# Hybrid decoder step: prompt's attention moved beside the sample's, the output projection beside the sample's products, the sample's dot products into the query stage

## Chip, cores and metric

One core of one Trainium2 chip runs the whole program. The metric is device time of one execution in microseconds (us); lower is better. Engines: PE (TensorE, matmuls and transposes), DVE (VectorE), ACT (ScalarE), POOL (GpSimd, which also issues the indirect gathers) and SP (SyncE, which issues all plain loads and stores).

## What is computed

One layer of a decoder over 256 prompt tokens and 8 x 4 sample tokens, all float32. Cut to what matters here:

```
proj = x @ w_in
y_r  = rwkv_time_mix(proj)        # 16 heads x 64, recurrence over tokens
y_n  = nsa_mix(proj)              # 16 query heads, 4 KV heads; compressed, selected, window; gated sum
x    = layer_norm(ALPHA * x + concat(y_r, y_n) @ w_out)
q    = x @ peer_wq                # then two top-16 searches over 128 keys, 16 experts a head
h    = gelu(x . u_tab[expert]);   f = sum(gate * h * v_tab[expert])
x    = layer_norm(ALPHA * x + f)
```

Prompt and sample do all of it with the same weights. The prompt's compressed, selected and window branches run over its own 256 keys, the sample's over 2048 cached tokens, gathered by page.

## The kernel before, in words

The program is one function, `hybrid_decode_step`. Its parts are Python generators that issue instructions and yield a cost; `weave((gen, weight), ...)` takes the next step of the generator that is furthest behind its weight, so parts are issued in turns. A scheduler of the framework then orders each engine's queue with a model of times, with the program's order as the priority. On the chip each queue runs in order. Tiles of one name share `bufs` slots; the first writer of a tile waits until the slot's last reader is done. PSUM has 8 banks, handed out by name: `banks(sa=2, sao=1, ...)`.

The stretches of the span (times in us from its start) that the change touches:

1. W3 (550 to 793): three parts woven. `late` is the sample's attention (30 of its 40 units of 256 keys each run here: transposes at L881 into bank `sa`, scores L894 into `pb`, softmax L898 to L908, transposes L913 into `pb`, values L921 into `sao`). `sample_states` and `sample_steps` (L1140 to L1270) are the sample's recurrence, bank `ss`. `take(prompt, NP3)` is 30 of the 84 steps of the prompt's recurrence (`prompt_steps`, L970 to L1133), bank `pa`. Cached keys come by gathers on POOL (L422, tile `co`) into a ring of 4 + NCX = 7 buffers.
2. W4 (793 to about 1117): again three parts woven. The prompt's last 18 steps; `prompt_attention` (L594 to L690), which for each half of the tokens (`qt`), each KV head (`kvh`) and each of its 4 query heads (`g`) makes scores for the selected and window branch (L654, bank `sa`), masks and takes maxima (L659), exponentiates (L664), transposes (L670, bank `sa`), copies (L672) and multiplies with values (L676, bank `sao`); after 4 heads the bank is scaled and added (L678 to L684). The results, transposed, go to `YN` (L690). `sample_chain` (L1386 to L1480): the sample's gates, its output projection (L1416, all 32 weight tiles of `w_out` read by themselves), layer norm, query product (L1416 again, `w_q`), choice of experts (`choose`, `settle`), and 64 gathers of 128 rows of `u_tab` (L422, tile `cw`, 5 buffers), each multiplied with x and summed: 52 on DVE (L1476), every fifth on POOL and ACT (L1473, L1474).
3. out (927 to 1182, overlapping W4): `out_part(0, BV)` and then `out_part(8, YN)`, the prompt's output projection. Each of 32 weight tiles is split into a high part (ACT, L1595) and a low part (DVE or POOL, L1596) and takes 12 matmuls (L1601, bank `pa`). Before it the prompt's gates (L1614, L1615).
4. ln1 (1182 to 1222): the prompt's layer norm, its transposes, stores of x.
5. wq (1222 to 1380): the prompt's queries (L1721) on PE. After each head, `choose` and `settle` on DVE (L1274 to L1327), with a product on POOL in them (L1320). The next stage (dense, L1744) writes `AW` (L1764), 128 KB per partition, where the tiles of wq were; its first write waits for the last `settle`.

Afterwards come dense (to 1855), weigh (to 2132) and V (to 2699). SBUF is a stack on a left and a right side: a pool opened after another has closed takes its place, so its first loads wait for the last reader there.

Of the kernel before, what the change touches and what calls it, by code (L numbers as in the profile page):

```python
# [38 lines left out]
OFFC = 5  # L39
# [5 lines left out]
NCX = 3  # L45
# [4 lines left out]
NP3 = 30  # L50
# [19 lines left out]
def _const_table():  # L70
# [23 lines left out]
    g5["bmask"] = bm  # L94
# [54 lines left out]
def hybrid_decode_step(ctx: ExitStack, tc: tile.TileContext, a, outs, dbg=None):  # L149
# [98 lines left out]
    KT = nq([P, 2, 2, NT], "KT")  # L248
    VS, VW = ([nq([P, 256], f"{nm}{t}") for t in range(2)] for nm in ("vs", "vw"))
# [343 lines left out]
    def prompt_attention():  # L593
# [12 lines left out]
        for qt in range(2):  # L606
# [39 lines left out]
            for kvh in range(4):  # L646
                kp, par = kvh // 2, kvh % 2
                po = bank("sao")
                su = np_([P, 4, 2], "su", bufs=2)
                for g in range(4):  # L650
                    yield 1
                    pb = bank("sa")
                    for br in range(2):
                        pe.matmul(pb[:, 256 * br:256 * br + nk], QT[hs[par], kp, g, tok], KT[hs[par], br, kp, :nk],  # L654
                                  start=True, stop=True)
                    Sm = np_([P, 2, 256], "Sm", bufs=2)
                    m2 = np_([P, 2], "m2", bufs=3)
                    for br in range(2):
                        ve.tensor_tensor_reduce(out=Sm[:, br, :nk], in0=pb[:, 256 * br:256 * br + nk],  # L659
                                                in1=C2("causal")[:, 256 - nk:256], scale=1.0, scalar=NEG,  # L660
                                                op0=OP.add, op1=OP.max, accum_out=m2[:, br:br + 1])
                    ve.tensor_scalar(m2, m2, -1.0, None, op0=OP.mult)
                    for br in range(2):
                        sc.activation(Sm[:, br, :nk], Sm[:, br, :nk], AF.Exp, bias=m2[:, br:br + 1],  # L664
                                      accum_out=su[:, g, br:br + 1])
                    pb = bank("sa")
                    for br in range(2):
                        for kt in range(qt + 1):
                            o = 256 * br + 128 * kt
                            pe.transpose(pb[:, o:o + 128], Sm[:, br, 128 * kt:128 * kt + 128], ident)  # L670
                    PTs = np_([P, 2, 256], "PTs", bufs=2)
                    sc.copy(PTs[:, :, :nk], pb.rearrange("p (a b) -> p a b", a=2)[:, :, :nk])  # L672
                    for br in range(2):
                        for kt in range(qt + 1):
                            o = 128 * g + 64 * br
                            pe.matmul(po[:, o:o + 64], PTs[:, br, 128 * kt:128 * kt + 128],  # L676
                                      (VS, VW)[br][kt][:, 64 * kvh:64 * kvh + 64], start=(kt == 0), stop=(kt == qt))
                ve.reciprocal(su, su)  # L678
                ve.tensor_tensor(su, su, Gt[:, 4 * kvh:4 * kvh + 4, 1:3], OP.mult)
                to = np_([P, 4, 2, 64], "to", bufs=2)  # L680
                ve.tensor_tensor(to.rearrange("p g r d -> p (g r) d"), po.rearrange("p (n d) -> p n d", n=8),
                                 su.rearrange("p g r -> p (g r)")[:, :, None].to_broadcast([P, 8, 64]), OP.mult)
                for br in range(2):
                    ve.tensor_tensor(O[:, 4 * kvh:4 * kvh + 4, :], O[:, 4 * kvh:4 * kvh + 4, :], to[:, :, br, :], OP.add)  # L684
            for q in range(2):
                pb = bank("sa")
# [473 lines left out]
    def sample_steps(sm):  # L1160
# [69 lines left out]
        for j in range(8):  # L1230
            pb = bank("ss")
            for h in range(2):
                uvm = sm([64, 8, 64], "uvm", bufs=2, tag="PR")
                gp.tensor_tensor(uvm, UVt[:, j, None, 64 * h:64 * h + 64].to_broadcast([64, 8, 64]),
                                 C5("bmask")[:64, :, None].to_broadcast([64, 8, 64]), OP.mult)
# [5 lines left out]
        for b in range(8):  # L1241
# [3 lines left out]
            S1 = sm([P, 4, P], "S1", bufs=2, tag="S0")  # L1245
# [10 lines left out]
        Yq, Yv = sm([P, 256], "Yq"), sm([P, 256], "Yv")  # L1256
# [4 lines left out]
        rsqrt(sm, Yq, Yv, "sg")  # L1261
# [123 lines left out]
    def sample_chain(cx):  # L1385
# [53 lines left out]
        x4, X1s = cx([P, D], "x4"), cx([P, 16, 32], "X1s")  # L1439
# [4 lines left out]
        for g in range(4):  # L1444
            sy.dma_start(x4[32 * g:32 * g + 32, :], X1D[NPR:NT, :])
# [16 lines left out]
        hd = cx([P, 2, 32], "hd")  # L1462
# [5 lines left out]
        for s_ in range(32):  # L1468
# [559 lines left out]
```

## Time and profile before

| what | us |
|---|---|
| median of 3 runs | 2686.79 |
| lowest, highest | 2673.55, 2705.59 |
| profiled execution: its own time | 2701.19 |
| profiled execution: span of its instructions | 2699.3 |

Busy over the whole span: PE 89%, DVE 73%, ACT 39%, POOL 49%. In the views below PE is the matmuls and PEld the weight loads beside them; PEclk is the granted clock of TensorE as a share of 2.4 GHz (0.5 is its lower level, 1.2 GHz). A PE that is busy in the records may still be slow, because matmuls overlap and because the clock is low.

### The profile page before, as it was taken

The numbers are of one execution on the slowest core, as the hardware profiler recorded it, in microseconds if no ns is written. First come the engines' busy times: TensorE is split into PE (matmuls) and PEld (weight loads), VectorE is DVE, ScalarE is ACT, GpSimd is POOL, SyncE is SP. The second block draws the span as 40 slices with busy tenths as digits, with TensorE's granted clock in tenths as the row PEclk, the third lists the DMA queues.
The fourth block names the chain that finished last, engine by engine and source line by source line (L and its number), as shares of the span: only waits on it lengthen the run. The fifth ranks groups of instructions, "written<-read, shape, count | busy, mean of one in ns | idle before, by whom it ended". The sixth has DMA issues, their size and how long they took to land.

```text
span 2699.3 us, 47864 instructions
## 1 busy us (share of the span) xinstructions
PE 2394.6 (89%) x17636; PEld 2005.0 (74%) x17636; DVE 1962.0 (73%) x4360; ACT 1046.3 (39%) x1958; POOL 1333.8 (49%) x1348
## 2 busy tenths in 40 slices
PE   6998899989879998659979999998679799999996
PEld 5877788756556656438879999997667588878885
DVE  3699864347533438784988887888986589888888
ACT  2443223332321323331134444443456544444543
POOL 3688642224210006763654444445556377767772
PEclk9999999978988588679989999998789899999998
DMA  5688866662647566777569999998668599999994
GB/s 170 197 262 261 242 201 188 222 187 101 210 149 269 158 209 222 257 253 207 168 218 351 352 350 346 348 352 276 225 213 298 193 336 321 328 341 321 328 322 176
DMA packets 346317, 683.49 MB, mean 253 GB/s; under 512 B 81230, under 2 KB 204443, under 8 KB 345019
## 3 DMA queue, kind: packets, MB, share of 16 engines
q1 hardware_dynamic: 251172, 344.67, 39.3%
q0 software_dynamic: 94912, 335.77, 35.4%
q8 instruction: 139, 2.28, 0.3%
q14 instruction: 94, 0.77, 0.1%
HBM read 664.77 MB, written 23.88 MB: 255 GB/s over the span
## 4 chain that ended last, share of the span: by engine, by line
PE 61%; DVE 14%; DMA 8%; issue 5%; POOL 3%; ACT 2%; SPq 1%; DVEq 0%; POOLq 0%; ACTq 0%
PE pb L1953 19%; PE ph L1762 13%; PE pt L1757 4%; PE pj L388 3%; PE pj L1721 2%; DVE rows L1687 2%; PE pa L1601 2%; PE pa L1002 1%; PE pa L1835 1%; PE sa L881 1%; PE fs L1853 1%; PE ss L1416 1%; PE px L1805 1%; PE pa L1059 1%; DMA co<-in_cache_sel_kv,sidx 1%
## 5 line engine op out<-in xcount | busy, mean ns | idle before, releaser
L422 POOL DMA_INDIRECT rows<-in_peer_u,gi x256 | 308.4, 1205 | 320.5 <-DVE rows L1687 284.4
L422 POOL DMA_INDIRECT rq<-in_peer_v,gi x256 | 374.9, 1464 | 171.6 <-issue 92.3
L1762 PE MATMUL ph<-XHd,uh 128*128 128x256 f32 x1024 | 306.5, 299 | 15.9 <-ACT AW L1764 15.9
L1687 DVE SCALAR_TENSOR_TENSOR rows<-rows,x1a 128x1024 f32<-128x1024 f32 x256 | 308.1, 1231 | 0.0
L1762 PE MATMUL ph<-XHd,ul 128*128 128x256 f32 x1024 | 297.5, 291 | 6.9 <-DVE ul L1574 6.9
L1762 PE MATMUL ph<-XLd,uh 128*128 128x256 f32 x1024 | 290.8, 284 | 0.0
L388 PE MATMUL pj<-XH,wl 128*128 128x288 f32 (+1 forms) x752 | 234.1, 312 | 33.1 <-DVE wl L383 17.2
L1573 ACT CAST uh<-pt 128x512 fp32r<-128x512 f32 x256 | 150.2, 587 | 271.8 <-PE ph L1762 271.0
L1574 DVE TENSOR_TENSOR ul<-pt,uh 128x512 fp32r<-128x512 f32 x256 | 176.5, 690 | 90.1 <-ACT uh L1573 86.9
L388 PE MATMUL pj<-XH,wh 128*128 128x288 f32 (+1 forms) x752 | 230.0, 306 | 7.6 <-DVE BV L767 4.8
L388 PE MATMUL pj<-XL,wh 128*128 128x288 f32 (+1 forms) x752 | 226.8, 302 | 0.0
L1953 PE MATMUL pb<-vl,ah 128*128 128x512 f32 x768 | 216.8, 391 | 1.3 <-DVE vl L1947 1.3
L1953 PE MATMUL pb<-vh,al 128*128 128x512 f32 x768 | 216.2, 390 | 0.0
L1953 PE MATMUL pb<-vh,ah 128*128 128x512 f32 x768 | 197.7, 393 | 18.6 <-ACT vh L1946 18.6
L1762 PEld LDWEIGHTS ph<-XHd,uh 128*128 128x128 f32 x1024 | 197.6, 193 | 16.2 <-ACT AW L1764 16.2
L1762 PEld LDWEIGHTS ph<-XHd,ul 128*128 128x128 f32 x1024 | 197.0, 192 | 7.6 <-DVE ul L1574 7.6
L1762 PEld LDWEIGHTS ph<-XLd,uh 128*128 128x128 f32 x1024 | 197.7, 193 | 0.0
L1927 DVE SCALAR_TENSOR_TENSOR fP<-rq,ge,fP 128x512 f32<-128x512 f32 x254 | 189.5, 746 | 4.3 <-DMA rq<-in_peer_v,gi 1.8
L381 ACT CAST wh<-wraw 128x512 fp32r<-128x512 f32 (+1 forms) x188 | 114.2, 616 | 185.5 <-PE pj L388 115.2
L1953 PEld LDWEIGHTS pb<-vh,ah 128*128 128x128 f32 x768 | 145.6, 190 | 49.5 <-ACT vh L1946 19.3
L388 PEld LDWEIGHTS pj<-XH,wl 128*128 128x128 f32 (+1 forms) x752 | 145.0, 193 | 49.0 <-DVE wl L383 24.4
L1953 PEld LDWEIGHTS pb<-vl,ah 128*128 128x128 f32 x768 | 144.8, 189 | 32.3 <-DVE vl L1947 2.1
(840 smaller groups left out, 5719.2 us busy)
## 6 DMA issues: line engine op xcount, KB each, us to landing
ur<-in_peer_u SPq DMA_DIRECT2D x128, 512.0 KB
wraw<-in_w_in SPq DMA_DIRECT2D x152, 256.0 KB
cw<-in_w_out SPq DMA_DIRECT2D x32, 512.0 KB
cw<-in_peer_wq SPq DMA_DIRECT2D x32, 512.0 KB
wraw<-in_w_out SPq DMA_DIRECT2D x32, 512.0 KB
wraw<-in_peer_wq SPq DMA_DIRECT2D x32, 512.0 KB
wraw<-in_w_in SPq DMA_DIRECT2D x64, 128.0 KB
co<-in_state_win_kv SPq DMA_DIRECT2D x16, 512.0 KB
```

The costliest lines, as they stand in the source:

```text
L381: sc.copy(wh[:, :, :n], w[:, :, :n])
L388: pe.matmul(pb[:n, :nt], wi[:, k, :n], xi[(o + k) // 8][:, (o + k) % 8, :nt], start=(o + k == 0 and wi is wh and xi is xh), stop=(o + k == ...
L422: gp.indirect_dma_start(out=dst, out_offset=None, in_=rows_, in_offset=bass.IndirectOffsetOnAxis(ap=ix, axis=0))
L1573: sc.copy(xh, pb)
L1574: return ve.tensor_tensor(xl, pb, xh.bitcast(F32), OP.subtract)
L1601: pe.matmul(acc[t], xi[:, e, P * t:P * t + P], wi[:, e, :], start=(k == e == n_ == 0), stop=(k == 6 and e == 1 and n_ == 2))
L1687: i_ = ve.scalar_tensor_tensor(r_, r_, 1.0, X1a[t], op0=OP.mult, op1=OP.mult, accum_out=h_)
L1721: pe.matmul(pb[:, :NPR], w[:, k, :], XT[:, o + k, :], start=(o + k == 0), stop=(o + k == 15))
L1757: pe.transpose(pb[:, 128 * e:128 * e + 128], w[:, 512 * q + 128 * e:512 * q + 128 * e + 128], ident)
L1762: mm = pe.matmul(ph[:, :NPR], wi[:, e, :], xi[:, 4 * q + e, :NPR], start=(q == 0 and e == 0 and wi is wh and xi is XHd), stop=(q == 1 and ...
L1927: ve.scalar_tensor_tensor(fP[t], r_, w_, fP[t], op0=OP.mult, op1=OP.add)
L1953: pe.matmul(acc[3 * t + q], wi[:, P * t:P * t + P], xi[:, 512 * q:512 * q + 512], start=(k == 0 and wi is ah and xi is vh), stop=(k == P - ...
```

## The change

W4 is gone. Its prompt recurrence and its prompt attention move into W3, its `sample_chain` is issued in turns with the output projection, and its 64 dot products become a part of their own, `sample_dots`, issued in wq.

```diff
-NCX = 3
-NP3 = 30
+NSC = 30
+NCX = 2
+    YN = QT.rearrange("p k g t -> p (k g) t")
...
-            for kvh in range(4):
-                kp, par = kvh // 2, kvh % 2
-                po = bank("sao")
-                for g in range(4):
-                    yield 1
-                    pb = bank("sa")
-                    for br in range(2):
-                        pe.matmul(pb[:, 256 * br:256 * br + nk], QT[hs[par], kp, g, tok], KT[hs[par], br, kp, :nk],
-                                  start=True, stop=True)
...
+            for kp in range(2):
+                for gh in range(2):
+                    yield 2
+                    po = bank("sao")
+                    for g2 in range(2):
+                        g = 2 * gh + g2
+                        bk = [bank("sa"), bank("sa")]
+                        for br in range(2):
+                            for par in range(2):
+                                pe.matmul(bk[par][:, 256 * br:256 * br + nk], QT[hs[par], kp, g, tok],
+                                          KT[hs[par], br, kp, :nk], start=True, stop=True)
...
+                        ve.tensor_scalar(m2, m2, -1.0, None, op0=OP.mult)
...
+                        for par in range(2):
+                            pb = bank("pb")
...
+        yield 1
...
-            for q in range(2):
-                r_, x_, h_ = ring(), x4[:, 1024 * q:1024 * q + 1024], hd[:, q, s_:s_ + 1]
-                gather(r_, uh2, (IG if q else GI[2])[:, s_:s_ + 1])
-                if (2 * s_ + q) % OFFC == OFFC - 1:
-                    gp.tensor_tensor(r_, r_, x_, OP.mult)
-                    sc.activation(r_, r_, AF.Copy, accum_out=h_)
-                else:
-                    ve.scalar_tensor_tensor(r_, r_, 1.0, x_, op0=OP.mult, op1=OP.mult, accum_out=h_)
...
+    def sample_dots(cd):
+        x4, hd = cd([P, D], "x4"), cd([P, 2, 32], "hd")
+        for g in range(4):
+            sy.dma_start(x4[32 * g:32 * g + 32, :], X1D[NPR:NT, :])
+        for i, (s_, q) in enumerate(todo):
+            while n < min(i + NCW, 64):
+                rows_[n] = cd([P, 1024], "cw", bufs=NCW)
+                gather(rows_[n], uh2, (IG if q1 else GI[2])[:, s1:s1 + 1])
+                n += 1
+            r_ = rows_.pop(i)
+            ve.scalar_tensor_tensor(r_, r_, 1.0, x4[:, 1024 * q:1024 * q + 1024], op0=OP.mult, op1=OP.mult,
+                                    accum_out=hd[:, q, s_:s_ + 1])
             yield 1
...
-    weave((late, 137 - NSA), (seq(sample_states(sx), sample_steps(sx)), 137 - NSA), (take(prompt, NP3), NP3))
+    weave((late, 137 - NSA), (seq(sample_states(sx), sample_steps(sx)), 137 - NSA), (prompt, 48), (prompt_attention(), 20))
...
-    banks(sa=3, sao=1, ss=2, pa=2)
-    weave((prompt, 80), (prompt_attention(), 36), (sample_chain(cx[0]), 70))
...
+    banks(ss=3, pa=5)
...
-    out_part(0, BV)
-    out_part(8, YN)
+    chain = sample_chain(cx)
+    weave((seq(out_part(8, YN), prompt_gates(), out_part(0, BV)), 36), (take(chain, NSC), NSC))
...
+    for _ in take(chain, 99):
+        pass
...
+    sdots = sample_dots(cd)
     for h in range(9):
         S = []
+        for _ in take(sdots, 99 if h == 8 else 32 if not h else 6):
+            pass
```

The banks of W3 stay sa=2, sao=1, pa=2, ss=1, pb=2. `prompt_attention` now does the two KV heads of one pair together, two query heads at a time, with its transposes in bank `pb`. `YN` takes the place of `QT`. `out_part(8, YN)` now runs first. 30 units of `sample_chain` (up to six of the eight blocks of its query product) are woven with the projection; the rest is issued behind ln1. Small tiles get other names and pools (`bmask`, `S1`, `Yq`, `Yv`, `to`).

## Rows read from the trace of the kernel before

**Rows 1.** Busy us by stage; columns: stretch, length, PE, PEld, DVE, ACT, POOL, PEclk, DMA, GB/s
```profile
550.00:793.00 243.00, 210.76 (x2628) 141.19 (x2628) 133.19 (x466) 78.90 (x219) 72.32 (x78) 0.87 0.52 163
793.00:911.00 118.00, 109.90 (x1166) 81.01 (x1168) 44.94 (x164) 22.87 (x78) 1.96 (x2) 0.73 0.58 190
911.00:1182.00 271.00, 228.09 (x1058) 153.94 (x1050) 172.22 (x366) 84.69 (x175) 126.61 (x93) 0.76 0.70 238
1182.00:1222.00 40.00, 12.17 (x48) 9.13 (x48) 31.45 (x64) 21.73 (x32) 17.13 (x12) 0.50 0.68 223
1222.00:1380.00 158.00, 133.49 (x661) 118.40 (x662) 124.91 (x567) 18.19 (x44) 87.58 (x144) 0.92 0.60 179
...
2132.00:2699.00 567.00, 527.30 (x2304) 435.05 (x2304) 490.20 (x499) 261.51 (x200) 374.87 (x256) 0.97 0.86 307
```

**Rows 2.** The same view, two stretches within W3
```profile
655.00:730.00 75.00, 71.67 (x903) 46.58 (x905) 40.73 (x117) 23.64 (x64) 27.02 (x30) 0.99 0.52 158
730.00:793.00 63.00, 43.48 (x535) 26.55 (x537) 34.78 (x142) 20.08 (x62) 17.36 (x17) 0.87 0.56 194
```

**Rows 3.** Chain that ended last, wq: start, length, what
```profile
1222.60 12.83 PE pj L1721 x48
...
1379.13 0.60 ACT AW L1764
```

**Rows 4.** Busy by PSUM tile: sa and sao over 793 to 1117, then pa
```profile
sum 324.00, PE 81.56 PEld 52.51 DVE 25.71 ACT 18.81; mean PE 40.78 PEld 26.25 DVE 12.85 ACT 9.40
...
sum 324.00, PE 37.02 PEld 33.13 DVE 5.46 ACT 0.00; mean PE 18.51 PEld 16.56 DVE 2.73 ACT 0.00
...
793.00:911.00 118.00, 45.77 (x690) 40.13 (x688) 14.76 (x26) 3.26 (x6) 0.73 0.58 190
```

**Rows 5.** Groups by line, 793 to 1117: count, busy us, mean ns, idle before
```profile
L654 PE MATMUL sa<-KT,QT 64*128 64x128 f32 (+1 forms) x128 | 37.6, 420 | 0.0
```

**Rows 6.** Timeline, PE then DVE, one block of the prompt's attention
```profile
838.12 0.43 PE L676 MATMUL sao<-vs,PTs 128*128 128x64 f32 x2
...
855.15 0.68 DVE L681 TENSOR_TENSOR to<-sao,su 128x512 f32<-128x512 f32 x1
```

**Rows 7.** Groups by line, POOL, 550 to 793: the gathers of cached keys
```profile
L422 POOL DMA_INDIRECT co<-in_cache_sel_kv,sidx x41 | 39.9, 974 | 80.7 <-PE sao L921 70.6 <-issue 4.1 <-PE ss L1227 2.4
```

**Rows 8.** Busy of line L1416 alone, 793 to 1040
```profile
sum 247.00, PE 49.01 PEld 13.34; mean PE 24.51 PEld 6.67
```

**Rows 9.** Groups by line, PE, 911 to 1182: the prompt's gates
```profile
L1614 PE MATMUL pa<-sg,wraw 128*128 128x256 f32 x16 | 9.2, 693 | 1.6 <-DMA cw<-in_peer_wq 1.6
```

**Rows 10.** Timeline of SP's queue as sample_chain begins
```profile
792.03 0.33 SPq L1351 DMA_DIRECT2D cw<-in_rwkv_g  x1
...
813.30 12.02 SPq L1414 DMA_DIRECT2D cw<-in_w_out  x9
```

**Rows 11.** Timeline of DVE: last query sum, first and last dot, first choice
```profile
999.37 0.42 DVE L1458 TENSOR_TENSOR qs<-qs,ss 128x256 f32<-128x256 f32 x1
...
1037.64 1.22 DVE L1476 SCALAR_TENSOR_TENSOR cw<-cw,x 128x1024 f32<-128x1024 f32 x1
...
1210.55 2.30 DVE L1476 SCALAR_TENSOR_TENSOR cw<-cw,x 128x1024 f32<-128x1024 f32 x1
...
1247.01 0.88 DVE L1274 MAX8 HV<-S 128x8 f32<-128x128 f32 x4 [31.02 <-ACT S L1294]
```

**Rows 12.** Groups by line: dots in 1030 to 1222, in dense, in wq
```profile
L1476 DVE SCALAR_TENSOR_TENSOR cw<-cw,x 128x1024 f32<-128x1024 f32 x52 | 70.7, 1374 | 18.4 <-DMA cw<-in_peer_u,ig 10.8 <-DMA cw<-in_peer_u,gi 7.5
...
L1687 DVE SCALAR_TENSOR_TENSOR rows<-rows,x1a 128x1024 f32<-128x1024 f32 x180 | 214.5, 1217 | 0.0
...
L1687 DVE SCALAR_TENSOR_TENSOR rows<-rows,x1a 128x1024 f32<-128x1024 f32 x11 | 16.7, 1535 | 0.0
```

**Rows 13.** Groups by line, POOL: wq's product, the dots' gathers in 1030 to 1222
```profile
L1320 POOL TENSOR_TENSOR hit<-hit,CE 128x864 f32<-128x864 f32 x16 | 39.9, 2515 | 0.1
...
L422 POOL DMA_INDIRECT cw<-in_peer_u,ig x32 | 40.7, 1271 | 21.7 <-DVE m L662 10.1 <-issue 5.2 <-ACT cw L1474 2.9
```

**Rows 14.** Busy of line L1476 alone in ln1
```profile
1182.00:1222.00 40.00, 10.86 (x16) 0.50 0.68 223
```

More of the change, by code (lines that the diff above doesn't have):

```diff
@@ L93, in _const_table @@
     bm[:64] = (np.arange(64)[:, None] % 8) == np.arange(8)[None, :]
-    g5["bmask"] = bm
+    c["bmask"] = bm
     c = g2
@@ L685, in prompt_attention @@
             for q in range(2):
-                pb = bank("sa")
+                pb = bank("pb")
                 for e in range(4):
@@ L1255, in sample_steps @@
         ve.scalar_tensor_tensor(Yf, pb[:, :256], -1.0 / 64, Yf, op0=OP.mult, op1=OP.add)
-        Yq, Yv = sm([P, 256], "Yq"), sm([P, 256], "Yv")
+        Yq, Yv = (sm([P, 256], nm, bufs=2, tag="tmp") for nm in ("Yq", "Yv"))
         sc.activation(Yq, Yf, AF.Square)
@@ L1438, in sample_chain @@
         norm_quarters(cx, x1s, gs_, bs_, "ss")
[L1439 removed]
+        X1s = cx([P, 16, 32], "X1s")
         for h in range(2):
@@ L1443, in sample_chain @@
                 sy.dma_start(X1D[NPR:NT, c_], x1s[32 * q:32 * q + 32, l_])
-        for g in range(4):
-            sy.dma_start(x4[32 * g:32 * g + 32, :], X1D[NPR:NT, :])
         turned(X1s, x1s)
@@ L1467, in sample_chain @@
         ve.tensor_scalar(IG, GI[2], 1.0, None, op0=OP.add)
-        for s_ in range(32):
-            for q in range(2):
-                r_, x_, h_ = ring(), x4[:, 1024 * q:1024 * q + 1024], hd[:, q, s_:s_ + 1]
-                gather(r_, uh2, (IG if q else GI[2])[:, s_:s_ + 1])
-                if (2 * s_ + q) % OFFC == OFFC - 1:
-                    gp.tensor_tensor(r_, r_, x_, OP.mult)
-                    sc.activation(r_, r_, AF.Copy, accum_out=h_)
-                else:
-                    ve.scalar_tensor_tensor(r_, r_, 1.0, x_, op0=OP.mult, op1=OP.mult, accum_out=h_)
+        yield 1
+    def sample_dots(cd):
+        x4, hd = cd([P, D], "x4"), cd([P, 2, 32], "hd")
+        for g in range(4):
+            sy.dma_start(x4[32 * g:32 * g + 32, :], X1D[NPR:NT, :])
+        todo, rows_ = [(s_, q) for s_ in range(32) for q in range(2)], {}
+        n = 0
+        for i, (s_, q) in enumerate(todo):
+            while n < min(i + NCW, 64):
+                s1, q1 = todo[n]
+                rows_[n] = cd([P, 1024], "cw", bufs=NCW)
[4 more added lines that the diff above has]
+                                    accum_out=hd[:, q, s_:s_ + 1])
             yield 1
@@ L1522, in hybrid_decode_step @@
     banks(sa=2, sao=1, pa=2, ss=1, pb=2)
+    np_ = Pool("np", "right")
+    for nm, shape, n_ in (("PTs", [P, 512], 2), ("Sm", [P, 512], 3), ("VcB", [P, 1024], 1),
+                          ("O", [P, 1024], 1), ("Sc", [P, P], 1), ("PcT", [P, P], 1), ("Gt", [P, 48], 1),
+                          ("mx", [P, 16], 1), ("sm_", [P, 16], 1), ("rc", [P, 16], 1), ("su", [P, 8], 2), ("m2", [P, 4], 3)):
+        np_(shape, nm, bufs=n_)
     co = Pool("co", "right")
@@ L1602, in out_part @@
                                       start=(k == e == n_ == 0), stop=(k == 6 and e == 1 and n_ == 2))
+                yield 1
             for t in range(2):
                 x_ = X1[t][cq // 2][:, c_]
-                if not o:
+                if o:
                     ve.scalar_tensor_tensor(x_, x_, ALPHA, acc[t], op0=OP.mult, op1=OP.add)
@@ L1608, in out_part, with prompt_gates @@
                     ve.tensor_tensor(x_, x_, acc[t], OP.add)
-    g2a, g2b = (oe([P, 1024], "wraw", bufs=4) for _ in range(2))
-    gate_rows(g2a, g2b)
-    for j in range(8):
-        pb = bank("pa")
-        pe.matmul(pb[:, :NPR], g2a[:, 128 * j:128 * j + 128], sg0[:, :NPR], start=True, stop=False)
-        pe.matmul(pb[:, :NPR], g2b[64:96, 128 * j:128 * j + 128], sg1[64:96, :NPR], start=False, stop=True)
-        ve.tensor_tensor(BV[:, j, :NPR], pb[:, :NPR], BV[:, j, :NPR], OP.mult)
-    out_part(0, BV)
-    out_part(8, YN)
+    def prompt_gates():
+        g2a, g2b = (oe([P, 1024], "wraw", bufs=4) for _ in range(2))
+        gate_rows(g2a, g2b)
+        for j in range(8):
+            pb = bank("pa")
+            pe.matmul(pb[:, :NPR], g2a[:, 128 * j:128 * j + 128], sg0[:, :NPR], start=True, stop=False)
+            pe.matmul(pb[:, :NPR], g2b[64:96, 128 * j:128 * j + 128], sg1[64:96, :NPR], start=False, stop=True)
+            ve.tensor_tensor(BV[:, j, :NPR], pb[:, :NPR], BV[:, j, :NPR], OP.mult)
+            yield 0.5
+    chain = sample_chain(cx)
+    weave((seq(out_part(8, YN), prompt_gates(), out_part(0, BV)), 36), (take(chain, NSC), NSC))
     rw.close()
     bp_.close()
+    cd = Pool("cd", "right")
     xq = Pool("xq", "right")
@@ L1740, in hybrid_decode_step @@
     xq.close()
+    cd.close()
     kq.close()
```

92 lines of the change are left out of this document (46 added, 46 removed).

## Prediction

> **What bounds the kernel now.** I read the busy time by stage first [rows 1], then short stretches of it, the chain that ended last, and the groups by line for prices. The reader is to see three different limits between 550 and 1380. In W3 the PE is busy 210.8 of 243 us at a granted clock of 0.87, no other engine passes 133 us. In the two stretches from 793 to 1182 PE is again the busiest (338 of 389 us) but at 0.73 and 0.76, so much of that is a slow clock; DVE has 217 us there. In wq, 1222 to 1380, PE stops early and DVE is busy 124.9 us; the chain starts there on PE's query product and ends with the dense stage's first write, L1764 at 1379.1, which has to wait for the last choice of experts [rows 3]. So the sum has three terms: the PE work up to the end of the projection, ln1, and the DVE work up to 1380. Nothing from 1380 on is edited; I take those 1319 us over unchanged.
>
> I express PE work in "full-clock us", its busy time times the granted clock of the stretch. W3 holds 210.8 x 0.87 = 183 of them in 243 us, so 60 us of room. Stretches show how far room can be filled: 655 to 730 is busy 71.7 of 75 at clock 0.99, while after 730, where the sample's recurrence has ended, PE falls to 43.5 of 63 [rows 2].
>
> **Part 1, W3 takes the rest of the prompt's recurrence and its attention.** Attention writes banks sa and sao: 81.6 + 37.0 = 118.6 us of PE between 793 and 1117 [rows 4], at about 0.735 that is 87 full-clock us. The 18 recurrence steps fill bank pa: 45.8 us at 0.73, 33 full-clock us [rows 4]. The new form puts the two KV heads' scores, 64 rows of the array each, next to each other in the queue in two banks. L654 costs 37.6 us [rows 5], 28 at full clock; if neighbours overlap fully half of it goes, 14, and if not at all nothing goes; I take the half. Added: 87 + 33 - 14 = 106. I let 20 of the 60 us of room be filled, since the new parts run until the stage's end where today's recurrence has stopped: W3 = 243 + 106 - 20 = about 330 us. Bounds: all room filled, 183 + 106 = 289, with the stage's first waits some 305; nothing filled, clock unchanged and no overlap of scores, 243 + 120 / 0.87 = 381. DVE's instructions on the moved parts' banks take 25.7 + 5.5 + 14.8 = 46 us [rows 4], with the small ones around them some 60, on top of its 133 in W3: 193 of 330. ACT has 79 us there today. Both stay beside PE.
>
> The attention now also shares banks with the sample's units. Bank sao has a single buffer. In one block of today it is held from the first value product at 838.1 to the scaling at 855.2, 17 us for four heads in a row [rows 6]. Two pairs should hold it for about one pair's latency, between 6 and 17 us; 12 x 8 blocks is 96 us in 330 in which no sample unit ends. Behind that wait stand the gathers of cached keys, which wait for sao's readers already now, 70.6 us, without being the bound [rows 7]. I count it at nothing, covered by the stage getting 87 us longer with the same 30 units; without this cover up to 96 us. The ring of one buffer less (7 to 6), the smaller tiles under other names and `YN` over `QT` (written when that half's scores are done) have the same cover.
>
> **Part 2, the projection beside the sample's products.** PE's work: 384 matmuls of 128 x 512, at V's pace, 527.3 us / 2304 = 0.229 [rows 1], 88 us; the sample's products 49.0 us at about 0.76, 37 full-clock us [rows 8]; the prompt's gates, 9.2 us for one of two passes [rows 9], about 10 us at full clock for both; the sample's gates and turned key tiles, some 8 (an estimate from the same kind of rows). Sum 143. At nine tenths full that is 159. Before it comes the start: all its pools lie where the sample's attention was, and SP issues 48 small loads ahead of the chain's first weights, 792.0 to 813.3, 21 us [rows 10]. 159 + 21 = 180 us. The other check is transfer: 32 + 32 + 24 tiles of 0.52 MB are 46 MB; at today's 238 GB/s [rows 1] 194 us, at V's 307 150 us. I stay at 180, bounds 150 and 215, the upper one with both streams held by SP's one in-order queue, where a load that waits for its buffer stops the other stream's load behind it. DVE's weight splits go here unchanged, beside PE.
>
> **Part 3, ln1, choice and the 64 dots.** Today the end of the projection (1182) to the first write of AW takes 198 us. The 64 dots leave the stretch 1038 to 1213 and DVE gets all of them, the 12 of POOL and ACT as well. Their price: 1.22 us alone in dense, 1.37 in 1030 to 1222, 1.54 in wq [rows 12], each with a read of the sum of 0.08; I take 1.45 together, 93 us. Ahead of them the chain's last two blocks of the query product (8 loads, about 16 us) and the choice: from the last query sum to the first dot it took 38 us [rows 11]. So dots begin 54 us behind the projection's end. The first choice of the prompt begins 65 us behind it and DVE idles 31 us before that [rows 11]: 11 us of the dots are free. In ln1 10.9 us of dots go [rows 14]; I count 8 of them as won. Hence 198 + 93 - 11 - 8 = 272 us. Bounds: 1.30 a dot and the whole idle gap used, 198 + 83 - 31 = 250; the upper end is rival C. POOL's queue gets 64 gathers of 1.27 us there, 81 us beside its 88 [rows 1, 13], 169 of 272, under DVE.
>
> What a rule says against this part: POOL's product in the choice reads SBUF for 2.5 us, 16 times [rows 13], and the dots cost 1.54 beside it where they cost 1.22 in dense [rows 12]; the last dot, beside POOL's layer norm, took 2.30 [rows 11]. The Trainium skill, SBUF — State Buffer, "Who interferes with whom", states that a DVE instruction with two SBUF inputs and a GpSimd instruction reading SBUF shut each other out for the whole instruction. By that rule, where each of the 32 dots among the choices met one product from its start, they would cost 32 x 2.5 = 80 us more; the trace agrees in direction, with 0.3 us a dot on average.
>
> **The sum.** Today 243 + 389 + 198 = 830 us from 550 to 1380. After: 330 + 180 + 272 = 782, 48 us less. The profiled execution took 2701.2 us (span 2699.3), 14 above the median of 2686.8; 2701.2 - 48 = 2653 on its scale, 2686.8 - 48 = 2639 on the median's, which I give.
>
> **The rivals.** A measurement tells about 1%, 27 us, from no change here.
>
> A, W3 fills up. With four parts PE always has something ready; W3 305, projection 165, last part 265: 735, 95 less, 2592. For it: 71.7 of 75 at 0.99 [rows 2]. Against: a start and an end of each stage stay, and the prompt's recurrence is a chain whose 18 steps took most of 118 us.
>
> B, the merged stages are no denser than the old. Bank sao is held through two contended latencies, the sample's units queue behind it and the clock stays low: W3 365, projection 200, 272: 837, about 7 more, 2694. For it: clock 0.73 to 0.76 from 793 on, with two or three parts woven [rows 1].
>
> C, the slower side: the dots go at their gathers' pace. Today 64 of them took from 1037.6 to 1212.9, 175 us or 2.74 each [rows 11], though DVE's share was 1.45. If five buffers and POOL's in-order queue hold them to that in wq, where each choice stands behind dots on DVE's queue, the last part is 198 + 175 - 19 = 354, the sum 864, 34 more, 2721. It decides from 0.75 us a dot above my 1.45. The locked port would come to the same place, 2719 by its 80 us. Against: in 1037 to 1213 DVE also did the projection and the attention; its idle time before dots was only 18.4 us [rows 12].
>
> D, nothing is gained since DVE's 93 us added in wq eat what PE gives: W3 350, projection 195, 280: 825, 2682.
>
> **How the numbers follow.** Forecast 0.50, A 0.10, B 0.14, C 0.16, D 0.10. Within the forecast's own range, 2612 to 2672, about nine tenths lie more than 1% faster; with A and a tenth of the others faster is 0.58. B and D and the rest of the forecast's upper end give 0.25 within 1%, C and the far end of B 0.17 slower. The range runs from A's 2592 to 2712, between B and C.
>
> **What would show it.** Right: in W3 one stage of 310 to 350 us with PE's clock above 0.9 and no fall in its last quarter; the projection and L1416 in one stretch of 170 to 190 us; in wq DVE busy nearly throughout, dots at 1.3 to 1.6 us, and some 272 us from the last L1608 or its like to the first L1764. Wrong at part 1: a clock of 0.75 in W3, the sample's values waiting long for sao. Wrong at part 2: PE idle before the projection's matmuls with SP waiting for a buffer. Wrong at part 3: DVE idle before dots with a gather as the releaser, or the first dot later than 54 us. A change of dense, weigh or V by more than a few us would be outside all of this.

## The result and the profile after

The changed kernel took 2722.1 us (median of 4 runs) beside 2686.0 for the kernel before on the same chip: a ratio of 1.012, with a 95% interval of 1.009 to 1.016. It is slower by 1.2%, clear of the spread; forecast were 2639 us and a chance of 0.58 for faster. The profiled span grew from 2699.3 to 2720.2 us, and all of that lies ahead of the first write of `AW` (L1764 before, L1794 now), which moved from 1379 to 1400 us. Behind it both kernels take 1320 us.

Busy time by stage of the changed kernel, with the columns of [rows 1]: W3, the projection, ln1, and wq up to the first write of `AW`.

```profile
550.00:927.00 377.00, 346.87 (x3819) 249.71 (x3819) 193.31 (x709) 129.74 (x395) 74.58 (x80) 0.83 0.33 101
927.00:1104.00 177.00, 149.49 (x811) 94.46 (x815) 64.68 (x105) 42.24 (x49) 19.09 (x8) 0.87 0.79 273
1104.00:1157.00 53.00, 30.63 (x261) 14.26 (x254) 25.82 (x100) 15.51 (x28) 8.21 (x12) 0.70 0.80 285
1157.00:1400.00 243.00, 142.15 (x661) 123.53 (x659) 211.75 (x718) 22.86 (x49) 180.78 (x217) 0.79 0.79 257
```

Forecast were 330, 180 and 272 (the last two lines together, from the projection's end at 1103.5). Measured are 377, 177 and 296. Parts 1 and 2 did shorten the way to the end of the projection: 554 us where [rows 1] have 243 + 118 + 271 = 632. Part 3 gave more than that back: 296 where it was 198.

W3 first. PE's work, busy time by granted clock, is 346.9 x 0.83 = 288 full-clock us, and 289 were forecast. The room beside it is 377 - 288 = 89 us, where W3 before had 60. PE stands idle for 377 - 346.9 = 30 us, as before (32); the rest is clock. A mean of 0.83 between the two levels, 0.5 and 1, means the lower one for 128 us of 377; before, at 0.87, it was 63 of 243. The same view for short stretches of W3, after the change, shows it at work:

```profile
700.00:713.00 13.00, 11.61 (x180) 8.77 (x176) 10.02 (x35) 3.12 (x9) 5.27 (x6) 1.00 0.70 210
713.00:716.00 3.00, 2.26 (x20) 1.90 (x21) 0.32 (x3) 2.90 (x11) 0.00 (x0) 0.93 0.33 56
716.00:746.00 30.00, 29.91 (x186) 23.77 (x184) 8.91 (x36) 7.21 (x22) 2.15 (x4) 0.50 0.26 40
746.00:757.00 11.00, 9.83 (x95) 6.34 (x94) 9.70 (x52) 6.48 (x23) 3.08 (x3) 0.97 0.72 206
757.00:780.00 23.00, 22.81 (x151) 18.63 (x154) 11.52 (x46) 5.98 (x21) 2.87 (x3) 0.50 0.17 63
```

From 716 to 746 PE is busy 29.9 of 30 us and makes 186 matmuls; in the 13 us ahead of 713 it made 180. A busy PE is here a PE at half its clock. The chain that ended last tells what stood ahead of that stretch (start, length, what):

```profile
667.10 0.33 SPq L868
667.50 38.94 issue
706.44 0.61 SPq L1260
...
708.45 4.55 DMA out<-S
...
713.10 0.59 ACT S L1257
...
713.74 0.66 PE ss L1255 x4
```

The sample's final states are copied by ACT (L1257) into two buffers (tile `S1`) and stored from there by SP (L1260). SP had issued its last window load (L868) at 667.4 and then stood for 39 us until the first state was copied, at 706.4. The third copy had to wait until the first store had landed, and PE, which fills the bank behind it, halted for 1.4 us at 712.4. That a halt stood ahead of the slow stretch doesn't yet show that it brought it.

In wq the answer to [rows 12] is this pair of groups on DVE: the 64 dots, and their price of 1.45 us together with the accumulator's read, are as forecast.

```profile
L1492 DVE SCALAR_TENSOR_TENSOR cw<-cw,x 128x1024 f32<-128x1024 f32 x64 | 87.2, 1366 | 16.3 <-DMA cw<-in_peer_u,ig 9.7 <-DMA cw<-in_peer_u,gi 6.4
...
L1321 DVE TENSOR_TENSOR CV<-HV 128x8 f32<-128x8 f32 (+3 forms) x81 | 11.7, 191 | 0.0
```

### The profile page after: what moved, and what is told of

It is laid out like the page before. It is cut to its first block, busy times and chain, and to the rows that moved or that the text cites. A ratio compares the mean times of both kernels' runs of the same rounds, so it can differ in the third digit from the quotient of the medians.

```text
span 2720.2 us, 47779 instructions
## 1 busy us (share of the span) xinstructions
PE 2367.7 (87%) x17636; PEld 1981.4 (73%) x17636; DVE 1952.7 (72%) x4368; ACT 1032.5 (38%) x1934; POOL 1315.1 (48%) x1336
## 4 chain that ended last, share of the span: by engine, by line
PE 51%; DVE 13%; issue 12%; DMA 9%; POOL 7%; ACT 2%; SPq 2%; POOLq 0%; DVEq 0%; ACTq 0%
PE pb L1983 18%; PE pj L388 5%; PE ph L1792 5%; POOL rows L422 5%; PE pa L1622 3%; DVE cw L1492 2%; DMA cw<-in_peer_wq 2%; DVE rows L1713 2%; PE pt L1787 1%; PE pa L1013 1%; PE pa L1865 1%; PE sa L892 1%; PE fs L1883 1%; DMA cw<-in_peer_u,gi 1%; DMA co<-in_cache_sel_kv,sidx 1%
```

## Experiments

Lengths of W3 are from 550 us to its last result, unless another start is named; "last part" is from the projection's end to the first write of `AW`. All edits are to the changed kernel. Several of them leave work out, so that they price a part and don't compute the layer. Of each edit the lines that matter are shown.

### What each part of W3 and the dots cost

```diff
-    sdots = sample_dots(cd)
+    sdots = iter(())                                   # e1_no_dots
-    weave(..., (prompt, 48), (prompt_attention(), 20))
+    weave(..., (prompt, 48))                           # e2_no_attention
+    weave(..., (take(prompt, 30), 30), (prompt_attention(), 20))  # e3_no_recurrence
+                if i > 9:                              # e4_double_keys, after L892
+                    for kp in range(2):
+                        for e in range(2):
+                            o = 256 * kp + 128 * e
+                            pe.transpose(pb[:, o:o + 128], tl[b2][:, e, 128 * kp:128 * kp + 128], ident)
```

> Left out: the sample's 64 dot products, their gathers and the scaling of the sample's gates by them. Theory 1, the dots cost what DVE needs for them, since DVE is the last to finish in the query stage: the last part, from the end of the projection to the first write of AW (296 us in the changed kernel), falls by 87 us of instructions and 5 of accumulator reads, to about 204, and the total by the same, to some 2630. Rival, they cost their transfers (the gathers stand beside the loads of w_q, and DVE waits for both): with the transfers gone the query product runs at its own pace and the part falls below 190. Second rival, they are mostly covered and the part is long because the chain ends behind ln1: it stays above 240.

> Left out: the prompt's attention in W3 (the projection multiplies the queries that stand in its place). W3 is 377 us in the changed kernel. Theory 1, PE's work at the clock it is granted is what W3 takes: the attention's 73 full-clock us go at 0.83, W3 falls by 88 to about 290. Rival, the bank sao and the scores' banks that the attention shares with the sample's units hold these up, beyond the attention's own work: W3 falls to 265 or less, which is 243 of the kernel before and some 20 for the 18 recurrence steps, and the units come evenly every 6 to 7 us.

> Left out: the last 18 of the 48 steps of the prompt's recurrence that W3 runs. Theory 1: 33 full-clock us of PE at 0.83, W3 falls from 377 by 40 to about 337. Rival, the attention and the sample's units are what is late, and the recurrence runs in their gaps: W3 stays above 360.

> Added: each of the sample's 30 units in W3 transposes its keys twice, into the same bank (240 more transposes of 128x128, 65 us at the 0.273 us that they take in the changed kernel). Theory 1, W3 is PE's work at a clock that does not change: W3 grows by 65 or more, to 440. Rival, W3 is a set of chains in which PE is kept waiting and its clock falls for that reason: the added work fills room and lifts the clock, W3 grows by less than 30, and the low-clock time falls from 131 us.

Without the dots the last part was 203 us, 93 less, and the time 2620.3. So they cost 93 in all; which resource they cost is a later question. Busy time, ln1 and wq of that run:

```profile
1092.00:1138.00 46.00, 31.45 (x260) 13.61 (x253) 25.41 (x99) 15.28 (x28) 8.03 (x11) 0.71 0.75 281
1138.00:1295.00 157.00, 131.91 (x662) 117.23 (x660) 133.33 (x590) 20.57 (x46) 92.40 (x153) 0.93 0.62 184
```

W3 without the attention:

```profile
550.00:822.00 272.00, 246.88 (x3310) 175.66 (x3310) 151.10 (x501) 83.83 (x227) 75.45 (x82) 0.87 0.49 141
```

W3 without the 18 steps of the recurrence:

```profile
550.00:896.00 346.00, 313.60 (x3123) 223.30 (x3121) 178.93 (x663) 125.63 (x387) 72.12 (x78) 0.79 0.36 108
```

W3 with the keys transposed twice:

```profile
550.00:949.00 399.00, 373.17 (x4061) 281.69 (x4060) 197.60 (x711) 132.29 (x397) 73.92 (x80) 0.83 0.32 95
```

The attention costs 377 - 272 = 105 us. Its work is 288 - 247 x 0.87 = 73, which is the forecast; 32 more are room: the low clock goes from 71 us (0.13 x 2 x 272) to 128, half of which is lost, and PE's idle time from 25 to 30. The recurrence's 18 steps cost 31 us for some 40 of work, so they do use about 9 us of room. The doubled transposes added 373 x 0.83 - 288 = 22 full-clock us (their single durations overlap, so 65 was the wrong sum in that expectation) and W3 grew by 22. Taken together nothing is won: the attention and the recurrence cost 105 + 31 = 136 us, and W3 grew by 377 - 243 = 134, for 106 of forecast work. Each of these is one run, and W3 with two store buffers varies by 7 us between runs of the same work (below).

### Bank or halt

```diff
-    banks(sa=2, sao=1, pa=2, ss=1, pb=2)
+    banks(sa=2, sao=2, pa=2, ss=1, pb=1)               # e5_two_sao
-            S1 = sm([P, 4, P], "S1", bufs=2, tag="PR")
+            if b % 4 == 0:                             # e8_s1_ring, e8b_s1_ring_again
+                S4 = sm([P, 4, 4, P], "S4", bufs=1, tag="big") if not b else None
+            S1 = S4[:, b] if b < 4 else sm([P, 4, P], "S1", bufs=2, tag="PR")
-                sy.dma_start(t_, src.rearrange("(p e) a h d -> p (e a h d)", e=2))
+                gp.dma_start(t_, src.rearrange("(p e) a h d -> p (e a h d)", e=2))  # e9_windows_on_pool
```

> In W3 bank sao gets a second buffer, which pb gives up (sao 2, pb 1). Theory 2, the one sao bank that the attention holds for 84 us in all keeps the sample's units and the gathers behind them waiting, and PE with them: W3 falls from 377 by 15 or more, and POOL's wait for sao's readers, 106.6 us, falls below 60. Rival, W3 is PE's work at the granted clock: the wait may fall, W3 stays within 10 of 377, or grows as pb has one buffer.

> The sample's final states are stored from six buffers instead of two (four of them in the place of a tile that is done by then), so that PE does not wait at 712 us for a store, 1.4 us, ahead of a stretch of 30.7 us at the low clock. Theory 4, a short halt of PE is what brings the low clock, which then lasts many times longer: the stretch from 716 to 746 is at the high clock, W3 falls by about 15. Rival, the clock is low for what PE has to do around there: another low stretch stands near it, the low-clock time stays near 130 us and W3 within 5 of 377.

> The changed kernel with the sample's window loads issued by POOL, whose queue holds the gathers into the same ring, instead of SP. Nothing else differs; the state stores keep their two buffers. Theory 4b, PE's halt at 712 us has its root in SP's in-order queue: a window load waits there 39 us for a buffer of the ring, which the change made one shorter, and the sample's state stores stand behind it; with the load elsewhere the halt and the low clock from 716 to 746 go, and W3 falls by 15 to 25, as with six store buffers (370 to 347 from the end of the shift state's copies). Rival, the six buffers helped for another reason (a different order of the instructions): W3 stays within 8 of the changed kernel.

> The changed kernel with six store buffers, the same as before, timed against the kernel before. Theory 4, the low clock that the halts bring is worth 15 to 20 us in W3: the ratio to the kernel before falls from 1.012 to 1.006 or less. Rival, the single run was low by chance (the same W3 took 347 to 363 us in the runs that hold it): the ratio stays at 1.010 or above.

With two buffers for `sao` (and one for `pb`) W3 took 390 us, and POOL's wait for the readers of `sao`, 106.6 us in the changed kernel, was 135.9. This arrangement does not help; whether `sao` alone would, with no bank taken from another, was not tried.

Six store buffers took 2685.4 us in a single run and 2692.7 as the median of ten, where the ratio to the kernel before is 1.003 (0.9996 to 1.0055). That is about four fifths of the 1.2%. W3 of the timed kernel, and then of the run with the chain wholly woven (further below), which has six buffers too:

```profile
550.00:901.00 351.00, 325.93 (x3811) 237.91 (x3811) 194.33 (x708) 130.09 (x394) 74.74 (x80) 0.87 0.35 106
550.00:927.00 377.00, 350.58 (x3854) 255.14 (x3854) 194.95 (x716) 132.95 (x401) 77.02 (x83) 0.81 0.34 103
```

The work is the same, 326 x 0.87 = 284; the low clock is 91 us instead of 128, and W3 is 26 shorter. In W3 with the attention in it the clock is then 0.87 again, as in the stage before the change. So the buffers gain time, but by what way is not shown, and not every run shows the gain: measured from the last copy of the shift state (L1531), four runs with six buffers and this W3 took 347, 346, 348 and 363 us, five with two buffers 369, 370, 370, 363 and 370. The run of 363 is the second line: the same work again, 351 x 0.81 = 284, but 143 us of low clock. Its clock is at 0.50 from 716 to 748 with PE busy all the time, as in the changed kernel, though PE's wait at the state copies ahead of it was 0.6 us. A halt of 1.4 us is thus not needed for that stretch, and the two stretches (757 to 780 has no halt over 1 us ahead of it either) stay without a shown cause.

With the window loads on POOL's queue W3 was 361 from that copy, 9 shorter, between the two answers expected; the total was 2714.9. That expectation took the 39 us on SP's queue for a window load's wait, with the stores behind it. In the trace above the load is out by 667.4 and the queue waits for the states themselves, so the edit did not touch what held the stores.

### What the dots take: DVE's time or their transfers

```diff
-    ve.scalar_tensor_tensor(r_, r_, 1.0, x4[:, 1024 * q:1024 * q + 1024], ...)
+    ve.scalar_tensor_tensor(r_[:, :8], r_[:, :8], 1.0, x4[:, 1024 * q:1024 * q + 8], ...)  # e7_gathers_alone
-    gather(rows_[n], uh2, ...)
+    rows_[n] = r0                                      # e13_products_alone, r0 set once
-    ve.scalar_tensor_tensor(r_, r_, 1.0, ...)
+    ve.scalar_tensor_tensor(r1, r_, 1.0, ...)
+            if i % 5 == 4:                             # e10_fifth_off, with six store buffers
+                gp.tensor_tensor(r_, r_, x_, OP.mult)
+                sc.activation(r_, r_, AF.Copy, accum_out=h_)
-NDW = 1
+NDW = 0                                                # e10_fifth_off
```

> The sample's 64 gathers stay in the query stage, each product and sum takes 8 columns instead of 1024 (the rest of the sample's dot products is left out). Theory 3, DVE's time is the price: the last part falls from 296 by about 70 to 225 or less. Rival, the gathers are the price, by their transfers beside w_q's loads and by POOL's queue: it stays above 265.

> The sample's 64 products and sums stay in the query stage at full size, on a constant tile; their gathers are left out, and with them the sample's dot products proper. Without both the last part took 203 us, with the gathers alone 262, with both 296. Theory 3, DVE's time is enough to set the stage's end: 64 x 1.45 come on top of a stage in which DVE has 24 idle us, the last part is 270 to 296. Rival, gathers and products each add a part: about 237, which is 203 and the 34 that the products added to the gathers.

> Six store buffers as before; besides, every fifth of the sample's 64 dot products is made by POOL and summed by ACT, as in the kernel before, and the query stage takes none of the prompt's dot products of its own accord (6 fewer). DVE loses 12 x 1.45 and 6 x 1.5, 26 us. Theory 3, DVE's time sets the stage's end: the last part falls from 295 by 20 to 26. Rival, the gathers' transfers set it: it falls by 10 or less, for the 3 MB that go with the prompt's.

The gathers alone made the last part 262 us, 59 of the 93. In wq of that run DMA is at 0.90 and 301 GB/s (in the run without dots at 0.62 and 184), while DVE works 148.5 of 208 us:

```profile
1093.00:1147.00 54.00, 28.47 (x266) 13.35 (x259) 26.06 (x98) 14.86 (x27) 8.04 (x11) 0.73 0.81 290
1147.00:1355.00 208.00, 139.56 (x664) 121.69 (x663) 148.50 (x722) 21.87 (x47) 149.04 (x217) 0.83 0.90 301
```

301 GB/s for 208 us are 62.6 MB, and 257 for 243 us are 62.5: the changed kernel moves the same bytes, and they fit in 208 us. Its other 35 us are DVE's: PE's query product has ended at 1297, and of the 103 us after that DVE is busy 96.9, with DMA at 0.65. The 262 lie just under the 265 that the rival asked for, and far over the 225 of theory 3.

The products alone made the last part 228 us, 25 more than without dots and under both answers expected. This is no clean price, because nothing holds them without their gathers: they began at 1094 us, ahead of the projection's end, and DVE was busy all 62 us of ln1 and 227 of the 228 us in all:

```profile
1104.00:1166.00 62.00, 32.26 (x244) 15.00 (x238) 62.00 (x150) 15.60 (x28) 10.08 (x11) 0.56 0.63 221
1166.00:1332.00 166.00, 131.37 (x661) 116.67 (x659) 165.35 (x656) 22.95 (x47) 97.45 (x153) 0.91 0.58 174
```

It does show that dots which wait for no gather, and so may begin earlier, cost a quarter of 93; how much of that is the start and how much the missing transfers, this run does not tell. In the changed kernel DVE has 25.8 + 211.8 = 238 busy us in a last part of 296, so 58 us of it are DVE standing idle.

With 18 dots fewer for DVE the last part was 301 us, no shorter (295 to 301 in the four other runs with six store buffers and all 64 dots on DVE in wq). DVE's busy time in wq was 211.6 us, as if nothing had been taken (211.75):

```profile
L1499 DVE SCALAR_TENSOR_TENSOR cw<-cw,x 128x1024 f32<-128x1024 f32 x52 | 76.6, 1476 | 18.9 <-DMA cw<-in_peer_u,ig 10.7 <-DMA cw<-in_peer_u,gi 8.0
L1323 DVE TENSOR_TENSOR CV<-HV 128x8 f32<-128x8 f32 (+3 forms) x81 | 23.8, 333 | 0.0
...
L1496 POOL TENSOR_TENSOR cw<-cw,x 128x1024 f32<-128x1024 f32 x12 | 28.2, 2350 | 1.3 <-DMA cw<-in_peer_u,gi 1.2
```

Beside POOL's 12 products the remaining dots took 1476 ns instead of 1366, and the small sums of L1321 (L1323 here) 333 instead of 191. The Trainium skill, SBUF — State Buffer, "Who interferes with whom", has DVE with two SBUF inputs and a reading POOL exclude each other; the trace agrees: 28.2 us of POOL's products stand against 52 x 0.11 + 12 = 18 us on these two groups, and the six small sums that took 1.7 to 3.1 us each ran beside a product of POOL.

The durations of single instructions also price the locked port in the changed kernel itself. Of its 64 dots in wq 59 took at most 1.26 us. The other five took 2.5 to 4.7 us, and each of them ran beside POOL's product in the choice (L1331). Over the others' 1.22 us they took 9 us together, not the 80 that the prediction worked out for 32 meetings.

### Three changes of order that gave little

```diff
+        yield from sample_dots(cx)                     # e6_dots_back: at the chain's end, none in wq
+    weave((seq(out_part(8, YN), ...), 36), (take(chain, 72), 72))
-            if b % 4 == 0:                             # e11_states_in_place, six store buffers
+            if not b:
                 S0 = sp([P, 4, 4, P], "big", bufs=1)
-    (take(chain, NSC), NSC)
+    (chain, 38)                                        # e12_chain_woven, six store buffers
```

> The sample's 64 dot products go back to the end of the sample's chain, beside the projection and the prompt's layer norm; nothing of them is left in the query stage; parts 1 and 2 of the change stay. Theory 3, the dots cost DVE's time in the query stage, where nothing covers them: from the start of the query product to the first write of AW it takes 157 us again (243 in the changed kernel), and in the stretch of projection and layer norm DVE has room for them (90 busy of 230 us); that stretch grows by the gathers' transfers, 64 x 0.52 MB at some 300 GB/s less what is free there, by 50 to 60; the total falls by about 30. Rival, the transfers are the price wherever they stand: the stretch grows by 90 or more, and the total is that of the changed kernel or above.

> Six store buffers as before; besides, the sample's states 4 to 7 are loaded into the tile of states 0 to 3 piece by piece, not as a new tile. In the run with six store buffers PE halts 5.6 us for such a load, and the clock is low from 590 to 621. Theory 4: the halt shrinks and the low stretch with it, W3 falls by 5 to 15 more. Rival: the load waits for something else and nothing changes, within 3.

> Six store buffers as before; besides, the whole of the sample's chain is issued in turns with the projection, where its last part was issued behind the layer norm. Theory: the first dot comes earlier than 68 us after the projection's end by 10 or more, the projection takes up to 15 longer, the time from the start of the projection to the first write of AW falls by 0 to 12. Rival: the transfers set the pace of the whole stretch and nothing is gained, or it grows.

With the dots at the chain's end, beside the projection as issued, they still ran from 1152 to 1265, because the chain's query product ended only at 1133: the last part was 329 us, and the time 2733 us, no gain but the rival's answer. States loaded in place: W3 342 us from the shift state's last copy, where the six buffers alone gave 347 and 346; no more than the spread. Chain wholly woven: the first dot stood 65 us behind the projection's end, as before (64), and the last part was 296. The order of issue alone does not make the chain earlier: its query product ended 45 us behind the projection's end (44 in the changed kernel), and PE waits there for loads of `w_q`.

### The same parts in another place

```diff
-    weave((late, 137 - NSA), (seq(sample_states(sx), sample_steps(sx)), 137 - NSA), (prompt, 48), (prompt_attention(), 20))
+    attention = prompt_attention()
+    weave((late, 137 - NSA), (seq(...), 137 - NSA), (take(prompt, A), A), (take(attention, B), B))
...
+    chain = sample_chain(cx)                           # with its 64 dots at its end
+    weave((prompt, 48 - A), (attention, 19 - B), (take(chain, N), N))
-    weave((seq(out_part(8, YN), prompt_gates(), out_part(0, BV)), 36), (take(chain, NSC), NSC))
+    weave((seq(out_part(8, YN), prompt_gates(), out_part(0, BV)), 36), (chain, C))
```

Between the two, the sample's pools are closed and `cx` is opened. A, B, N, C are 34, 13, 19, 83 (v1), 30, 10, 30, 72 (v2) and 22, 6, 38, 66 (v3), all with six store buffers and with no dots issued in wq.

> Six store buffers; W3 is issued so that the sample's attention and recurrence end when 34 of 48 steps of the prompt's recurrence and 13 of 19 of the attention's are issued, and the sample's chain begins beside the rest of these two; the 64 dot products stand at the end of the chain again, beside the projection. Theory 5, the dots' 93 us are the price of a stage in which DMA (0.93 of its time with the gathers) and DVE are both full, while DMA moved 101 GB/s in W3: the last part falls to about 200, W3 with the chain's start stays near 370, the projection takes 190 to 210 with the gathers; the first write of AW comes 60 to 85 us earlier, the total is 2640 to 2660. Rival, the chain's loads and the dots slow the attention and the projection by as much: 2690 or more.

> The same with the sample's parts ending at 30 of 48 and 10 of 19, and 30 units of the chain, into its query product, beside the rest of the prompt's parts. Theory 5: within 15 of the version before it, earlier dots and a shorter projection against a slower attention. Rival: 2690 or more.

> The version that took 2674.8 us in one look, timed against the kernel before. Theory 5: its ratio to the kernel before is 0.993 to 0.998, with the last part near 227. Rival, the look was a low one: the ratio is 1.000 or above.

> The sample's attention and recurrence end when 22 of 48 steps of the prompt's recurrence and 6 of 19 of its attention's are issued; the whole chain up to the choice of experts, 38 units, is issued beside the rest of these, so that the loads of w_q no longer stand alone (in the version before it PE was busy 38 of 61 us between the end of the attention and 1024 us, at a clock of 0.64, with DMA at 0.93); only the 64 dot products stand beside the projection. Theory 5: first dot before 1010 us, the query stage takes 157 to 165 us again, the first write of AW comes at 1325 to 1340 (1355 in the version before it), the total is 2645 to 2660, ratio 0.985 to 0.991. Rival, the chain's loads slow the attention by as much: ratio 0.995 or above.

The first took 2687.2 us, ratio 1.001 (0.998 to 1.004): not what was expected (2640 to 2660 us); its first dot came at 1090 and its wq still took 201 us. The second took 2674.8 in a single run and 2679.9 as a median of twelve, ratio 0.998 (0.996 to 1.000). The third took 2662.9 us, ratio 0.991 (0.988 to 0.9945): faster than the kernel before by 24.5 us, at the slow end of what was expected. Six store buffers alone had 1.003, so the new places give 1.1% more. The profiled run took 2648.6 us, 14 less than the median, and the kernel before was profiled 14 us over its own, so the stages show more gain than the times do. The stages: W3 to the end of the sample's units, the chain beside the rest of the prompt's parts, the projection with the dots, ln1, wq.

```profile
550.00:804.00 254.00, 216.90 (x2517) 143.66 (x2515) 133.96 (x482) 85.06 (x257) 66.39 (x73) 0.85 0.46 139
804.00:967.00 163.00, 155.63 (x1738) 113.11 (x1739) 69.03 (x247) 45.24 (x143) 6.08 (x6) 0.86 0.68 226
967.00:1119.00 152.00, 121.69 (x576) 86.91 (x574) 128.98 (x234) 41.30 (x49) 91.19 (x68) 0.91 0.88 310
1119.00:1162.00 43.00, 11.51 (x50) 9.51 (x51) 41.01 (x84) 13.59 (x21) 28.66 (x23) 0.52 0.81 280
1162.00:1325.00 163.00, 134.27 (x660) 118.30 (x658) 134.09 (x582) 22.61 (x48) 88.58 (x147) 0.92 0.63 194
```

The chain's loads run at 226 GB/s beside the attention, where W3 of the changed kernel moved 101; DVE has the dots in the projection (129 of 152 us) and ln1; wq is 163 us again, 80 less than in the changed kernel. From 550 to the first write of `AW`, at 1325, it is 775 us, where the changed kernel took 850 and the timed one with six buffers 821.

## Why the prediction was wrong

**What bounds the kernel.** The reading by three limits held: PE's work, and then wq. What it left out is DMA in wq, which [rows 1] show at 0.60 before the change, with 0.4 of 158 us, 63 us, free and 64 gathers of 0.52 MB to come, which at 301 GB/s are 111 us.

**Part 1, work.** The sum is right: 289 full-clock us forecast, 288 measured; the attention's 73 (87 less the 14 of paired scores) is what leaving it out gave. Its parts are in part luck. The paired scores took 25.7 us of PE where [rows 5] have 37.6; at the mean clocks of their stages that is 21 and 28 at full clock, so about 7 were saved and not 14. And leaving out the recurrence's steps took off some 40, where 33 were counted.

**Part 1, room.** The step that failed first: "I let 20 of the 60 us of room be filled". None was; the room grew to 89. W3 took 377 instead of 330, the end that was named as the bound with nothing filled, 381. Of the 47 us too many about 20 are the filling that did not come: with six store buffers W3 took 351, and 243 + 106 is 349. The other 26 are clock that those buffers gave back in the timed version. The stretch at 0.99 in [rows 2] was read as a sign that a fuller PE keeps its clock, and it belonged to other work. That the attention brings a low clock with it (it had run at 0.73 to 0.76 [rows 1]) is not shown either: without it the low clock was 71 us and with it 128, but with it and six store buffers 84 to 143. What sets the clock within W3 stays open.

**Part 1, what was costed at nothing.** "The smaller tiles under other names" and the shorter ring were to be covered by a longer stage. With six store buffers in place of two the ratio went from 1.012 to 1.003. That is a gain beyond the kernel before, which has two as well and lost 0.6 us of PE to them; no run here prices the new names or the shorter ring. The hold on `sao` was costed at nothing too. Here the runs don't speak against it: the attention's 105 us are explained by work and clock, and the version with two buffers, one taken from `pb`, was slower.

**Part 2.** Right in its length: 180 us forecast, 177 measured, with DMA at 273 GB/s, between the two rates of its check by transfers. Some of that is luck: of the 143 full-clock us 149.5 x 0.87 = 130 ran there. The rest of the sample's query product ran on into ln1, 18.2 us of PE.

**Part 3.** The second step that failed. The sum was 198 + 93 - 11 - 8 = 272. The 93 came out, as 296 - 203, but for other reasons: 59 come with the gathers alone. The rest without dots was 203, not 198, and the 19 us of cover didn't come, which makes the 24 us that the sum was short: the first dot stood 64 us behind the projection's end, not 54, and ln1 grew from 40 to 53. The transfers of 33 MB, which had been hidden in stretches with DMA at 0.70 [rows 1], were given no term.

**The rivals.** W3 went as in B (365) and beyond. Rival C had the right side and half of the mechanism: the gathers set much of the pace, though not at 2.74 us a dot (the 64 ran from 1168 to 1385, with choices between them). That its 2721 us meets the measured 2722 is luck: it stands on a W3 of 330 and a last part of 354, where 377 and 296 were measured. The same holds for the 2719 of the locked port. The port is real, as the run with a fifth of the dots on POOL shows, but in wq of the changed kernel it cost 9 us on the dots.

**The balance.** 377 + 177 + 296 = 850 where the kernel before took 830: about 20, and the spans differ by 21. Forecast were 782.

## What to carry to other kernels

Price a moved part at no less than its own work at full clock: idle time and low clock in the stage that it enters are no room for it until a run shows that something was filled. Here 106 us of work, as forecast, cost 108 (351 - 243) in the timed version with six store buffers and 134 in the changed kernel, so the price of the work alone was already the good case. For each moved part write down its bytes as well as its engine time, and the DMA share of the stage it leaves and of the one it enters; here 33 MB left a stage with room and came to one that had too little, while 101 GB/s ran where more than 300 could. And when parts depend on each other, it is the start of the longest chain that has to move: the same dots were worth 80 us of wq once the chain ahead of them began beside the attention.

## What was not expected of the hardware

W3 with the same work to within 2% took 346 to 370 us over the nine runs listed above, and the difference is the granted clock (91 us at 1.2 GHz in the timed version with six buffers, 128 in the changed kernel, 143 in the run of 363). The four runs with six buffers hold one of 363 among three of 346 to 348. About 30 us at the lower level, with PE busy all but 0.1 us, stood behind a halt of 1.4 us in one run and of 0.6 us in another; what brings them is not shown.

Taking 18 products from DVE and giving 12 of them to POOL left DVE as busy as it was, 211.6 us, because the rest got slower. A product on DVE beside one on POOL took 2.5 to 4.7 us in wq of the changed kernel, where the other 59 took at most 1.26.
